# A down product of seven block products in four chunks, with the final norm at the end, and the first norm's root by groups

## The chip, the cores and the metric
One Trainium2 chip; the kernel runs on one of its cores. The metric is the device time of one execution in microseconds (us). The engines are TensorE (PE in the profile, PEld its weight loads), VectorE (DVE), ScalarE (ACT), GpSimd (POOL) and SyncE (SP), which only issues DMAs. DMAs go out from the queues of SP and of POOL.

## What is computed
One step of a hybrid encoder layer for 640 tokens (512 of a prompt, 8 streams of 16), width 2048, feed-forward width 5632:

```python
h = rmsnorm(x, norm1_g)
x = x + concat(GLA(h @ W_in), GatedDeltaNet(h @ W_in), RWKV7(h @ W_in)) @ W_out
h = rmsnorm(x, norm2_g)
x = x + (silu(h @ W_gate) * (h @ W_up)) @ W_down
y = rmsnorm(x, final_norm_g)        # y_prompt, y_sample
```

Everything is float32, and the mixers' states are outputs as well. Each large product is made in float32 by three matmuls: an operand is split into a part `hi`, which ACT copies in a rounded format, and the rest `lo`, which DVE subtracts; the product is hi·hi + hi·lo + lo·hi.

## The kernel before, in words
`build` (L1358) runs the stages one behind another. `norm1` (L1433) loads five tiles of 128 tokens, squares each on ACT, takes its root on DVE (`rsq`, twelve small operations), scales it on DVE (L1453 to L1457) and turns it on PE (L1464), so that features lie on partitions. `mixers` is ordered by a planner of its own, which the change does not touch. `outproj1` and `outproj2` multiply by `w_out`; in `outproj2` the sum x2 is kept feature-major, its squares feed the second norm, and `rows` (L1580) turns it on PE and stores it token-major in DRAM (`x2d`). From there on the tile scheduler fixes each engine's order; `high_priority(offset=WPRIO)` puts weight preparation ahead.

`gateup` (L1723) makes the gate and up products. Each of 21 pairs of matrices (256 columns) is made from seven block products in place of eight (Strassen and Winograd's scheme: the four quarters of the weights and of the activations, with four sums of each, `S1` to `S4` and `T1` to `T4`), 24 matmuls of 128x320 each (`pw`, L1736 to L1738); the first pair is made by the dense `first`. The products are added on DVE (L1744, L1779, L1784), and the activations s, 44 blocks of 128 features by 640 tokens, go to DRAM (`actd`).

`down` (L1795) multiplies them by `w_ffn_down` in five chunks of 9, 9, 9, 9 and 8 feature blocks. For each chunk it loads and splits the activations (L1811, L1812); for each of four column blocks of 512 it splits the weights (`split`, L1321, L1322) and runs the three matmuls of 128x512 per feature block and token tile (L1835 to L1837), 2,640 in all, into eight PSUM banks; DVE adds each bank to y in SBUF (L1839). In the last chunk ACT squares y as each column block is done (L1842), POOL multiplies three column blocks by the norm's weight (L1845), and for the last column block the order goes by token tile, so that root, scaling and the outputs of a tile (L1847 to L1858) follow while PE works on the next.

Of the kernel before, what the change touches and what calls it, by code (L numbers as in the profile page):

```python
# [11 lines left out]
F32 = mybir.dt.float32  # L12
# [8 lines left out]
T = 640  # L21
# [1264 lines left out]
class Trunk:  # L1286
# [10 lines left out]
    def split(self, src, shape, fill=None, keep=False):  # L1297
# [12 lines left out]
        with self.tc.high_priority(offset=WPRIO):  # L1310
# [5 lines left out]
            if keep:  # L1316
                hi, lo = (self.fb.tile(shape, F32R, name=self.name("k" + x), tag="k" + x, bufs=5) for x in ("h", "l"))
            else:
                hi = self.wp.tile(shape, F32R, name=self.name("hi"), tag="hi", bufs=NHL)
                lo = self.wp.tile(shape, F32R, name=self.name("lo"), tag="lo", bufs=NHL)  # L1320
# [39 lines left out]
    def build(self):  # L1360
        tc, nc, a, o = self.tc, self.nc, self.a, self.o
        ctx = ExitStack()
        with ctx:
            self.wp = ctx.enter_context(tc.tile_pool(name="wp", bufs=1))
# [7 lines left out]
            x2d = dp.tile([NT, 128, D], F32, name="x2d")  # L1372
            actd = dp.tile([44, 128, T], F32, name="actd")
            mctx = ExitStack()
            bp = ctx.enter_context(tc.tile_pool(name="bp", bufs=1, side="right"))
            self.free, self.where = [(bp, f"b{i}") for i in range(32)], {}
# [13 lines left out]
            self.px = ctx.enter_context(tc.tile_pool(name="px", bufs=1, space=PSUM))  # L1390
            with tc.tile_pool(name="fa", bufs=1) as self.fa:
                self.outproj2(KORDER[8:], xs, x2, self.col("norm2_g"), x2d, actd)
                self.gateup(actd)
            with tc.tile_pool(name="fb", bufs=1) as self.fb:
                self.down(actd, x2d)
# [27 lines left out]
    def norm1(self, h):  # L1423
        tc, nc, a = self.tc, self.nc, self.a
        with tc.tile_pool(name="xp", bufs=1) as xp, tc.tile_pool(name="xps", bufs=2, space=PSUM) as xps:
# [27 lines left out]
            for i in range(NT):  # L1453
                with tc.high_priority():
                    nc.scalar.activation(junk, xs[i], AF.Square, accum_out=ssq[:, i:i + 1])
                    r = self.rsq(xp, ssq[:, i:i + 1], 1, 1.0 / D)
                    nc.vector.tensor_scalar(xs[i], xs[i], r, None, ALU.mult)  # L1457
# [97 lines left out]
    def outproj2(self, ks, xs, x2, g2, x2d, actd):  # L1555

        nc, a, fa, px = self.nc, self.a, self.fa, self.px
# [21 lines left out]

        def rows(hf, q):  # L1580

            for t0, t1 in cuts[hf]:
                n, t = t1 - t0, 320 * hf + t0
                p = self.pe.tile([128, 512], F32, name=self.name("yt"), tag="e")
                for j in range(4):
                    nc.tensor.transpose(p[0:n, j * 128:(j + 1) * 128], xv[4 * q + j][:, t:t + n], self.ident)
# [307 lines left out]
```

## Time and profile before

| | us |
|---|---|
| three runs: median (lowest, highest) | 3337.22 (3337.09, 3342.08) |
| profiled execution, its own time | 3333.61 |
| its span | 3331.5 |
| PE busy | 3283.1 |
| DVE busy | 2037.4 |
| ACT busy | 1226.7 |
| POOL busy | 186.6 |
| clock granted to PE, mean | 0.994 |

The span runs from the first to the last instruction of the profiled execution. Busy time of an engine that others do not wait for costs nothing by itself. A matmul's record is longer than its place in the queue, since matmuls overlap.

### The profile page before, as it was taken

Reading aid. Unit: us, or ns where it says so; the run is one execution under the profiler, and the core shown is the slowest. Engines: PE = TensorE matmul, PEld = TensorE weight load, DVE = VectorE, ACT = ScalarE, POOL = GpSimd, SP = SyncE. Lnnn points to the kernel's source line nnn. Section 1 sums busy time; section 2 is a strip of 40 time slices with the busy share of each in tenths; the row PEclk is TensorE's granted clock in tenths of the full one; section 3 lists DMA queues with packets and bytes.
Section 4 is the critical chain, followed back from the end, with each engine's and each line's share of the span. In section 5 each row is a group of like instructions: output and inputs, shape, how many; then the busy total and the mean of one; then the engine's idle time right before and its main releaser. Section 6 shows DMA issues by size and latency. Waiting matters only on the chain.

```text
span 3331.5 us, 58063 instructions
## 1 busy us (share of the span) xinstructions
PE 3283.1 (99%) x22453; PEld 3042.1 (91%) x22453; DVE 2037.4 (61%) x5209; ACT 1226.7 (37%) x2593; POOL 186.6 (6%) x332
## 2 busy tenths in 40 slices
PE   6999999999999999999999999999999999999998
PEld 6988888899899999999999999999999988888886
DVE  5677577645666666426887777777777753233335
ACT  4433333323333334335543444444444332122123
POOL 1111111000100000002000000000000000000001
PEclk9999999999999999999999999999999999999999
DMA  4221121122222224435533333333323363233223
GB/s 127 57 52 49 45 52 42 49 59 75 75 73 72 76 73 134 131 106 176 146 99 93 100 102 100 98 97 105 105 85 105 105 215 105 83 108 98 80 83 114
DMA packets 357016, 312.08 MB, mean 94 GB/s; under 512 B 24161, under 2 KB 313427, under 8 KB 355971
## 3 DMA queue, kind: packets, MB, share of 16 engines
q1 hardware_dynamic: 347794, 287.97, 29.5%
q0 software_dynamic: 8656, 20.40, 2.1%
q8 instruction: 175, 2.87, 0.4%
q14 instruction: 103, 0.84, 0.1%
q10 hardware_dynamic: 288, 0.01, 0.0%
HBM read 271.32 MB, written 36.98 MB: 93 GB/s over the span
## 4 chain that ended last, share of the span: by engine, by line
PE 93%; DVE 3%; DMA 2%; ACT 1%; issue 1%; SPq 0%; ACTq 0%; DVEq 0%
PE d_r L292 23%; PE pw L1736 10%; PE pw L1737 10%; PE pw L1738 10%; PE mm_r L292 10%; PE dn L1835 6%; PE dn L1837 6%; PE dn L1836 6%; PE pd L1338 3%; PE pd L1339 3%; PE pd L1340 3%; PE ma_r L292 2%; PE po_r L292 1%; PE pd L1539 1%; DMA b<-mixd 0%
## 5 line engine op out<-in xcount | busy, mean ns | idle before, releaser
L292 PE MATMUL d_r<-b,hi_r 128*128 128x320 f32 (+1 forms) x3648 | 807.3, 319 | 0.7 <-ACT b L1471 0.7
L292 PEld LDWEIGHTS d_r<-b,hi_r 128*128 128x128 f32 (+1 forms) x3648 | 598.8, 189 | 23.9 <-issue 15.5
L292 PE MATMUL d_r<-b,lo_r 128*128 128x320 f32 (+1 forms) x1824 | 511.2, 319 | 0.0
L1322 DVE TENSOR_TENSOR lo<-raw,hi 128x512 fp32r<-128x512 f32 x299 | 210.3, 704 | 457.0 <-ACT hi L1321 441.8
L1736 PE MATMUL pw<-b,hi 128*128 128x320 f32 x1416 | 437.6, 309 | 0.0
L1737 PE MATMUL pw<-b,hi 128*128 128x320 f32 x1416 | 437.5, 309 | 0.0
L1738 PE MATMUL pw<-b,lo 128*128 128x320 f32 x1416 | 437.2, 309 | 0.0
L1321 ACT ACTIVATE hi<-raw 128x512 fp32r<-128x512 f32 x299 | 188.6, 631 | 540.0 <-PE dn L1837 388.8
L1835 PE MATMUL dn<-hi,b 128*128 128x512 f32 x855 | 338.5, 396 | 0.1
L1836 PE MATMUL dn<-lo,b 128*128 128x512 f32 x855 | 337.1, 394 | 0.4 <-DVE lo L1322 0.4
L1837 PE MATMUL dn<-hi,b 128*128 128x512 f32 x855 | 337.1, 394 | 0.0
L292 PEld LDWEIGHTS d_r<-b,lo_r 128*128 128x128 f32 (+1 forms) x1824 | 326.3, 189 | 10.8 <-issue 6.5
L1736 PE MATMUL pw<-b,hx 128*128 128x320 f32 x936 | 289.5, 309 | 0.0
L1737 PE MATMUL pw<-b,hx 128*128 128x320 f32 x936 | 289.2, 309 | 0.0
L1738 PE MATMUL pw<-b,lx 128*128 128x320 f32 x936 | 289.2, 309 | 0.0
L292 DVE TENSOR_TENSOR lo_r<-raw_r,hi_r 128x512 fp32r<-128x512 f32 (+1 forms) x228 | 155.3, 682 | 182.0 <-ACT hi_r L292 121.0
L1736 PEld LDWEIGHTS pw<-b,hi 128*128 128x128 f32 x1416 | 266.0, 188 | 0.4 <-ACT b L1576 0.2
L1737 PEld LDWEIGHTS pw<-b,hi 128*128 128x128 f32 x1416 | 266.1, 188 | 0.2
L1738 PEld LDWEIGHTS pw<-b,lo 128*128 128x128 f32 x1416 | 266.0, 188 | 0.0
L292 ACT ACTIVATE hi_r<-raw_r 128x512 fp32r<-128x512 f32 (+1 forms) x228 | 142.1, 624 | 243.4 <-PE d_r L292 206.9
L1338 PE MATMUL pd<-b,hi 128*128 128x320 f32 x640 | 201.0, 315 | 3.9 <-ACT s L1675 2.7
L1339 PE MATMUL pd<-b,hi 128*128 128x320 f32 x640 | 198.7, 311 | 0.4 <-DVE b L1514 0.4
(465 smaller groups left out, 5756.6 us busy)
## 6 DMA issues: line engine op xcount, KB each, us to landing
raw_r<-in_w_in SPq DMA_DIRECT2D x224, 256.0 KB
raw<-in_w_ffn_down SPq DMA_DIRECT2D x176, 256.0 KB
rw<-in_w_ffn_gate SPq DMA_DIRECT2D x84, 512.0 KB
rw<-in_w_ffn_up SPq DMA_DIRECT2D x84, 512.0 KB
raw<-in_w_out SPq DMA_DIRECT2D x80, 256.0 KB
actd<-s SPq DMA_DIRECT2D x88, 160.0 KB
b<-actd SPq DMA_DIRECT2D x44, 320.0 KB
mixd<-G_r POOLq DMA_DIRECT2D x16, 320.0 KB, 2.5
```

Of the source, the lines that this page charges most:

```text
L292: self.made.append(op[2](*op[3], **op[4]))
L1321: nc.scalar.activation(hi, raw, AF.Copy)
L1322: nc.vector.tensor_tensor(lo, raw, hi.bitcast(F32), ALU.subtract)
L1338: nc.tensor.matmul(out, lhsT=hi[:, kk, :], rhs=xh, start=k == 0, stop=False)
L1339: nc.tensor.matmul(out, lhsT=hi[:, kk, :], rhs=xl, start=False, stop=False)
L1340: nc.tensor.matmul(out, lhsT=lo[:, kk, :], rhs=xh, start=False, stop=k == nk - 1 and not extra)
L1736: nc.tensor.matmul(ps, lhsT=hi[:, kk, :], rhs=bh, start=k == 0, stop=False)
L1737: nc.tensor.matmul(ps, lhsT=hi[:, kk, :], rhs=bl, start=False, stop=False)
L1738: nc.tensor.matmul(ps, lhsT=lo[:, kk, :], rhs=bh, start=False, stop=k == 7)
L1835: nc.tensor.matmul(pds[i], lhsT=ah, rhs=hi, start=j == 0, stop=False)
L1836: nc.tensor.matmul(pds[i], lhsT=ah, rhs=lo, start=False, stop=False)
L1837: nc.tensor.matmul(pds[i], lhsT=al, rhs=hi, start=False, stop=j == len(fs) - 1)
```

## The change
`down` is written anew by the scheme of `gateup`. The 22 pairs of feature blocks are cut into four chunks of 5, 6, 6 and 5; per chunk and per block of 256 output columns (eight) seven products of 15 or 18 matmuls of 128x320 are made, 3,696 matmuls in all. The four quarters of the result are added by DMAs that accumulate into `yd`, feature-major in DRAM, where `outproj2` has stored x2 (32 stores; `rows` is gone). In the last chunk `load` and `turned` bring each finished block back, turn it on PE, square it on ACT and multiply it by the norm's weight on DVE. After the last block come one root for all five token tiles, 20 scalings and all 20 outputs.

The activations are stored as seven operands (four sums added by `store_sums`), loaded from POOL's queue two units at a time, and split in units of 128x320 by `Acts`, three products ahead of their use. Its first loads begin in the last up matrix, as each of that matrix's operands is given back.

In `norm1` the root is taken for tiles (0), (1, 2) and (3, 4) together, and the last tile is scaled on ACT. The pool `wp` moves and is closed before `down`; the tiles of `tq` and `s` live in a pool `fs` through the end.

```diff
-            for i in range(NT):
+            for i0, i1 in ((0, 1), (1, 3), (3, 5)):
                 with tc.high_priority():
...
+                    for i in range(i0, i1):
+                        nc.scalar.activation(junk, xs[i], AF.Square, accum_out=ssq[:, i:i + 1])
+                    r = self.rsq(xp, ssq[:, i0:i1], i1 - i0, 1.0 / D)
+                    for i in range(i0, i1):
+                        if i < NT - 1:
+                            nc.vector.tensor_scalar(xs[i], xs[i], r[:, i - i0:i - i0 + 1], None, ALU.mult)
+                        else:
+                            nc.scalar.activation(xs[i], xs[i], AF.Copy, scale=r[:, i - i0:i - i0 + 1])
...
+                nc.sync.dma_start(out=yd[m][:, c], in_=xv[m][:, c])
...
-                if m % 4 == 0 and m:
-                    rows(hf, m // 4 - 1)
...
+    def store_sums(self, m, s):
...
+        sub(t3, s[3], s[1])
+        sub(s[1], s[1], s[0])
+        sub(s[3], s[3], s[1])
+        sub(s[0], s[2], s[3])
+        for x, t in (("T3", t3), ("T1", s[1]), ("T2", s[3]), ("T4", s[0])):
+            nc.sync.dma_start(out=self.acts.at(x, m), in_=t)
...
+        def used(x):
+            self.give(*self.places[x])
+            self.acts.step(True)
...
+    def down(self, yd):
...
+        for n, (p0, p1) in enumerate(CHUNKS):
...
+                def split(x):
+                    hi, lo = tile("dh", F32R, pool=fw), tile("dl", F32R, pool=fw)
+                    nc.scalar.activation(hi, A[x], AF.Copy)
+                    nc.vector.tensor_tensor(lo, A[x], hi.bitcast(F32), ALU.subtract)
+                    return hi, lo
...
+                def product(parts, x):
...
+                    B = acts.take(n, x)
+                    for k in range(c):
+                        bh, bl = B[k][:, 0:320], B[k][:, 320:640]
+                        nc.tensor.matmul(ps, lhsT=hi[:, k], rhs=bh, start=k == 0, stop=False)
+                        nc.tensor.matmul(ps, lhsT=hi[:, k], rhs=bl, start=False, stop=False)
+                        nc.tensor.matmul(ps, lhsT=lo[:, k], rhs=bh, start=False, stop=k == c - 1)
...
+                with early():
+                    t1 = tq()
+                    d11 = split("11")
+                    total("S1", "21", "22", ALU.add)
+                    total("S2", "S1", "11", ALU.subtract)
+                    s2 = split("S2")
+                nc.scalar.activation(t1, product(d11, "11"), AF.Copy)
+                acts.step(p == 7)
...
+                u2, u4 = tq(), tq()
+                plus(u2, t1, product(s2, "T2"))
+                acts.step(p == 7)
...
+            def turned(p, y):
+
+                junk = tq()[:, 0:256]
                 for i in range(NT):
...
+                    ps = self.px.tile([128, 512], F32, name=self.name("yt"), tag=("st", "y")[i % 2])[:, 0:256]
+                    for j in range(2):
+                        nc.tensor.transpose(ps[:, 128 * j:128 * j + 128], y[j].bitcast(F32)[:, 128 * i:128 * i + 128], self.ident)
+                    nc.scalar.activation(junk, ps, AF.Square, accum_out=ssq[:, i, p:p + 1])
...
+                    nc.vector.tensor_tensor(rows[i, p // 2][:, 256 * (p % 2):256 * (p % 2) + 256], ps,
+                                            gf[p // 2][:, 256 * (p % 2):256 * (p % 2) + 256], ALU.mult)
...
+                def done(i, x, y):
+                    z = tq() if i == 3 else x
+                    plus(z, x, y)
+                    if last and p == 7:
+                        out = yl[i // 2].bitcast(F32)[:, ones(i)]
+                        plus(out, out, z)
                     else:
...
+                        nc.gpsimd.dma_start(out=yd[2 * p + i // 2][:, ones(i)], in_=z, accum_op=ALU.add)
...
+            turned(7, yl)
+            tot = fb.tile([128, NT], F32, name="ytot")
+            nc.vector.tensor_reduce(tot, ssq, AX.X, ALU.add)
+            r = self.rsq(fb, tot, NT, 1.0 / D)
...
+class Acts:
...
+    def step(self, many=False):
+
+        self.now += 1
+        free = self.trunk.free
+        for i in range(3):
+            if self.loaded and free and self.loaded[0][0] <= self.now - 7:
+                self.split()
+        soon = self.now + 3 - self.begin
+        if soon >= 0:
+            n, x = divmod(soon, 56)
+            if x < 7 and n < len(CHUNKS):
+                self.make(n, OPS[x])
+        for i in range(4 if many else 1):
+            if self.next < len(self.units) and len(free) > 2 and len(self.loaded) < (14 if many else 4):
+                self.load()
...
+CHUNKS = ((0, 5), (5, 11), (11, 17), (17, 22))
```

The order on ACT at the seam from `gateup` to `down`; before, the splits of the down product's activations (L1811) stand among weight splits of the last up matrix (`hi`, `hx`, L1710):

```order
L1710 ACTIVATE hi_28361<-rw_28235 128x512 [waits DMAHW7_49,PE_49,Activation_49]
L1811 ACTIVATE b_28523<-b_28525 128x640 [waits DMAHW4_49]
L1710 ACTIVATE hi_28393<-sx_28327 128x512 [waits DVE_49,PE_49,Activation_49]
L1811 ACTIVATE b_28529<-b_28531 128x640 [waits DMAHW5_49]
L1710 ACTIVATE hx_28397<-sx_28329 128x512 [waits DVE_49,PE_49,Activation_49]
L1811 ACTIVATE b_28535<-b_28537 128x640 [waits DMAHW6_49]
L1710 ACTIVATE hx_28431<-raw_28253 128x512 [waits PE_49,Activation_49]
```

With the change, the activation splits (L2001) stand ahead of the weights of the first products (`dh`, L1857; `dh_28597` is the first product's weight, `dh_28605` the second's):

```order
L1857 ACTIVATE dh_28597<-dr_28592 128x640 [waits DMAHW0_49]
L2001 ACTIVATE b_28899<-b_28721 128x320
L2001 ACTIVATE b_29267<-b_29086 128x320 [waits DVE_49]
L2001 ACTIVATE b_29080<-b_28902 128x320 [waits DMASW6_49,PE_49]
L2001 ACTIVATE b_29083<-b_28902 128x320 [waits PE_49]
L2001 ACTIVATE b_29110<-b_28932 128x320 [waits DMASW7_49]
L2001 ACTIVATE b_29113<-b_28932 128x320
L1857 ACTIVATE dh_28605<-ds_28603 128x640 [waits DVE_49]
L1857 ACTIVATE dh_28643<-ds_28601 128x640
L1857 ACTIVATE dh_28683<-dr_28594 128x640 [waits DMAHW2_49,PE_49,Activation_49]
L1886 ACTIVATE t_28596<-dn_28609 128x320 [waits PE_49]
```

The weight split of the second product moved behind four activation splits, two of which wait for transfers.

The order on DVE at the end of the program. Before, the last token tile's addition, reduce and root follow the scaling of the tile ahead of it:

```order
L1849 SCALAR_TENSOR_TENSOR b_28601<-b_28601,q_32823,gfrow 128x512 [waits DVE_49]
L1852 TENSOR_SCALAR b_28591<-b_28591,q_32823 128x512 [waits Pool_49]
L1839 TENSOR_TENSOR b_28603<-b_28603,dn_32567 128x512 [waits PE_49]
L1847 TENSOR_REDUCE yssq<-yssq 128x1 [waits Activation_49]
L1476 TENSOR_SCALAR q_32847<-yssq 128x1 [waits DVE_49]
L89 TENSOR_SCALAR q_32848<-q_32847 128x1 [waits DVE_49]
```

With the change, the last additions (L1826) and multiplications of turned tiles (L1941) stand ahead of one reduce (L1960) and one root for all tiles:

```order
L1941 TENSOR_TENSOR b_35049<-yt_35045,b_33443 128x256 [waits Activation_49]
L1826 TENSOR_TENSOR b_34898<-b_34898,t_34906 128x320 [waits DVE_49]
L1941 TENSOR_TENSOR b_35025<-yt_35070,b_33443 128x256 [waits Activation_49]
L1941 TENSOR_TENSOR b_35031<-yt_35075,b_33443 128x256 [waits Activation_49]
L1941 TENSOR_TENSOR b_35037<-yt_35080,b_33443 128x256 [waits Activation_49]
L1941 TENSOR_TENSOR b_35043<-yt_35085,b_33443 128x256 [waits Activation_49]
L1941 TENSOR_TENSOR b_35049<-yt_35090,b_33443 128x256 [waits Activation_49]
L1960 TENSOR_REDUCE ytot<-yssq 128x5
L1482 TENSOR_SCALAR q_35097<-ytot 128x5 [waits DVE_49]
```

The scaling of every tile moved behind the last product.

The order on ACT in norm 1, from the square of the fourth tile on, before and now (`x_129` is the last tile, `hi_r` a weight of the first mixer):

```order
L1455 ACTIVATE xjunk,xssq<-x_127 128x2048 [waits DMAHW1_49,Activation_49]
L1455 ACTIVATE xjunk,xssq<-x_129 128x2048 [waits DMAHW2_49,Activation_49]
L292 ACTIVATE hi_r_394<-raw_r_393 128x512 [waits DMAHW3_49]
L1471 ACTIVATE b_74<-xpa_234,cols_106 128x640 [waits PE_49]
L1471 ACTIVATE b_76<-xpa_242,cols_106 128x640 [waits PE_49]
```

```order
L1457 ACTIVATE xjunk,xssq<-x_127 128x2048 [waits DMAHW1_49,Activation_49]
L1457 ACTIVATE xjunk,xssq<-x_129 128x2048 [waits DMAHW2_49,Activation_49]
L1463 ACTIVATE x_129<-x_129,q_184 128x2048 [waits DVE_49,Activation_49]
L293 ACTIVATE hi_r_362<-raw_r_361 128x512 [waits DMAHW3_49]
L1477 ACTIVATE b_74<-xpa_202,cols_106 128x640 [waits PE_49]
```

The scaling of the last tile moved from DVE to ACT, ahead of the first weight's split.

## Rows read from the trace of the kernel before

**Rows 1.** The page: the span, PE's busy time, the chain's shares by engine.
```profile
span 3331.5 us, 58063 instructions
...
PE 3283.1 (99%) x22453; PEld 3042.1 (91%) x22453; DVE 2037.4 (61%) x5209; ACT 1226.7 (37%) x2593; POOL 186.6 (6%) x332
...
PE 93%; DVE 3%; DMA 2%; ACT 1%; issue 1%; SPq 0%; ACTq 0%; DVEq 0%
```

**Rows 2.** Table by stretches: start:end, us, busy time (count) by engine, PEclk, DMA share, GB/s.
```profile
2200.00:2600.00 400.00, 400.00 (x2727) 400.00 (x2726) 295.44 (x504) 163.85 (x275) 0.00 (x0) 1.00 0.33 100
...
2820.00:3220.00 400.00, 400.00 (x1720) 322.88 (x1719) 135.92 (x204) 89.22 (x139) 0.00 (x0) 1.00 0.30 93
...
3321.00:3324.00 3.00, 0.46 (x2) 0.02 (x1) 1.59 (x8) 1.01 (x3) 0.00 (x0) 1.00 0.82 299
```

**Rows 3.** PE's timeline at both ends of the down product: start us, us, line, operation.
```profile
2703.94 0.31 PE L1738 MATMUL pw<-b,lo 128*128 128x320 f32 x1
...
2704.08 0.40 PE L1835 MATMUL dn<-hi,b 128*128 128x512 f32 x1
...
3321.06 0.40 PE L1837 MATMUL dn<-kh,b 128*128 128x512 f32 x1
```

**Rows 4.** PE's timeline in the second out-projection, around twelve transposes.
```profile
1495.21 0.31 PE L1340 MATMUL pd<-b,lo 128*128 128x320 f32 x1
...
1495.36 1.47 PE L1586 MATMUL yt<-ident,b 128*128 128x128 f32 x12
...
1496.97 0.31 PE L1340 MATMUL pd<-b,lo 128*128 128x320 f32 x1
```

**Rows 5.** Timelines of ACT, DVE and PE in norm 1, its last tile.
```profile
16.52 1.91 ACT L1455 ACTIVATE xjunk<-x 128x2048 f32<-128x2048 f32 x1 [0.55 <-DMA x<-in_x_sample]
...
24.56 1.29 DVE L1457 TENSOR_SCALAR x<-x,q 128x2048 f32<-128x2048 f32 x1
...
25.91 0.69 PE L1464 MATMUL xpa<-ident,x 128*128 128x128 f32 x2 [2.82 <-DVE x L1457]
```

**Rows 6.** Timelines of DVE, ACT and SP after the last matmul.
```profile
3323.03 0.16 DVE L1847 TENSOR_REDUCE yssq<-yssq 128x1 f32<-128x4 f32 x1 [0.85 <-ACT yjunk L1842]
...
3325.53 0.72 ACT L1850 ACTIVATE b<-b,q 128x512 f32<-128x512 f32 x1 [2.53 <-DVE q L94]
...
3326.28 1.95 SPq L1858 DMA_DIRECT2D out_y_sample<-b  x4
```

**Rows 7.** Timelines of POOL and DVE where both work, in two stretches.
```profile
213.49 0.56 POOL L292 DMA_DIRECT2D mixd<-G_r  x1 [3.03 <-DVE G_r L292]
...
213.72 0.68 DVE L292 TENSOR_TENSOR KB_r<-a_r,a_r 128x512 f32<-128x512 f32 x1
...
3233.23 3.07 DVE L1839 TENSOR_TENSOR b<-b,dn 128x512 f32<-128x512 f32 x5
...
3234.76 7.22 POOL L1845 TENSOR_TENSOR b<-b,gfrow 128x512 f32<-128x512 f32 x5 [520.28 <-ACT yjunk L1842]
...
3236.22 1.64 DVE L1322 TENSOR_TENSOR lo<-raw,hi 128x512 fp32r<-128x512 f32 x1
```

**Rows 8.** DMA issues: transfer, queue, count, KB each, median us to landing.
```profile
mixd<-G_r POOLq DMA_DIRECT2D x16, 320.0 KB, 2.5
...
Ss_r<-in_state_gdn POOLq DMA_DIRECT2D x6, 512.0 KB, 5.0
```

**Rows 9.** DVE and ACT by line and form: count, busy us, mean ns.
```profile
L1744 DVE TENSOR_TENSOR tq<-tq,pw 128x320 f32<-128x320 f32 x98 | 47.7, 487 | 43.6 <-PE pw L1738 43.3
...
L1322 DVE TENSOR_TENSOR lo<-raw,hi 128x512 fp32r<-128x512 f32 x138 | 95.3, 691 | 279.9 <-ACT hi L1321 279.8
...
L1812 DVE TENSOR_TENSOR b<-b,b 128x640 fp32r<-128x640 f32 x28 | 23.1, 825 | 41.1 <-ACT b L1811 41.0
...
L1811 ACT ACTIVATE b<-b 128x640 fp32r<-128x640 f32 x28 | 20.7, 738 | 43.6 <-DMA b<-actd 43.2 <-DVE b L1812 0.3
```

More of the change, by code (lines that the diff above doesn't have):

```diff
@@ L1 @@
 import heapq
+import itertools
 import math
@@ L1315, in split @@
                 nc.sync.dma_start(out=view, in_=ap)
[L1316 to L1320, printed above, removed]
+            hi = self.wp.tile(shape, F32R, name=self.name("hi"), tag="hi", bufs=NHL)
+            lo = self.wp.tile(shape, F32R, name=self.name("lo"), tag="lo", bufs=NHL)
             nc.scalar.activation(hi, raw, AF.Copy)
@@ L1578, in split @@
             ops[x].append(out)
[L1580 to L1586, printed above, removed]
-                row = self.take()
-                nc.scalar.activation(f(row)[0:n, 0:512], p[0:n], AF.Copy)
-                nc.sync.dma_start(out=x2d[t // 128][t % 128:t % 128 + n, q * 512:(q + 1) * 512], in_=f(row)[0:n, 0:512])
-                self.give(row)
         def first(k):
@@ L1652, in outproj2 @@
             split(new("T2"), v[:, H], "T2")
-        self.first(actd)
+        self.first()
         self.give(*b12)
@@ new lines, with __init__, at, load @@
+class Acts:
+    def __init__(self, trunk, actd):
+        self.trunk, self.actd = trunk, actd
+        self.units = [(n, x, p) for n, (p0, p1) in enumerate(CHUNKS) for x in OPS for p in range(p0, p1)]
+        self.now, self.next, self.loaded, self.made = 0, 0, [], {}
+        self.begin = 7
+    def at(self, x, p):
+        return self.actd[[u[1:] for u in self.units].index((x, p))]
+    def load(self):
+        i = self.next
+        self.next += 2
+        place = self.trunk.take()
+        raw = place.bitcast(F32).rearrange("p (q c) -> p q c", q=2)
+        self.trunk.nc.gpsimd.dma_start(out=raw, in_=self.actd[i:i + 2].rearrange("q p c -> p q c"))
+        for q in range(2):
+            self.loaded.append((self.now, *self.units[i + q][:2], raw[:, q], place if q else None))
+    def split(self):
+        nc = self.trunk.nc
+        at, n, x, raw, place = self.loaded.pop(0)
+        t = self.trunk.take()
+        hi, lo = t[:, 0:320], t[:, 320:640]
+        nc.scalar.activation(hi, raw, AF.Copy)
+        nc.vector.tensor_tensor(lo, raw, hi.bitcast(F32), ALU.subtract)
+        self.made.setdefault((n, x), []).append(t)
+        if place is not None:
+            self.trunk.give(place)
+    def step(self, many=False):
[12 more added lines that the diff above has]
+                self.load()
+    def make(self, n, x):
+        p0, p1 = CHUNKS[n]
+        while len(self.made.get((n, x), [])) < p1 - p0:
+            if not self.loaded:
+                self.load()
+            self.split()
+    def take(self, n, x):
+        self.make(n, x)
+        return self.made[n, x]
+    def used(self, n, x):
+        self.trunk.give(*self.made.pop((n, x)))
```

230 lines of the change are left out of this document (138 added, 92 removed).

## The prediction
> **What bounds the kernel now.** I read the page first. PE is busy 99% of a span of 3331.5 us, DVE 61%, and the chain of waits is 93% PE [rows 1]: a change pays by what it takes off PE's queue, and costs where another engine makes PE wait. The table by stretches then gives a price per matmul. In 400 us of the gate and up products PE issues 2727 matmuls of 128x320, 0.1467 us each; in 400 us of the down product 1720 of 128x512, 0.2326 us each [rows 2]. Both are full queues, PE busy the whole 400 us at clock 1.00, so start-to-start is the price (the records' own lengths overlap). PE's timeline gives the ends of the stage: the last `pw` starts at 2703.94, the first `dn` 0.14 us later, the last `dn` at 3321.06 [rows 3]. The stage is 617.1 us, and 2,640 x 0.2326 = 614.1 fills it: down has nearly no stalls to win back, only matmuls.
>
> **The down product.** The order has 3,696 matmuls of 128x320 in place of 2,640 of 128x512: 8 output blocks x 7 products x 22 pairs x 3. At 0.1467 that is 542.2, so **-71.9 us**. The price is that of the gate and up stage, whose form is the same (three matmuls per 128x128 weight, 320 columns). Bounds: 0.1467 in that stage, and 0.1454 if 0.2326/512 held per column (-76.8).
> The Trainium skill (TensorE: Matmul & The Clock Gate, "Back-to-back issue gap") gives sustained spacings of about 81 ns at 128 columns and 131 ns at 512, that is a large part that does not shrink with the columns, which speaks against cutting matmuls narrower. The two rows here, 147 ns and 233 ns, lie 0.45 ns per column apart with some 3 ns left over [rows 2], so the trace does not agree.
>
> **Transposes taken from the second out-projection.** `rows` turns x2 there: 96 transposes. In PE's timeline twelve stand between the matmuls that start at 1495.21 and 1496.97 [rows 4]; of these 1.76 us three matmuls of 0.147 take 0.44, so twelve transposes take 1.32, 0.11 us each. **-10.6 us**. The 24 ACT copies went beside matmuls; 32 stores on SP replace 24, no load waits for them.
>
> **Norm 1.** x's last tile is squared at 16.52 on ACT, but its root waits behind tile 3's on DVE, and its scaled form comes at 24.56 + 1.29; PE's last such wait is 2.82 us, ended at 25.91 [rows 5]. With tiles 3 and 4 in one root, twelve operations at 0.19 us from about 18.6 follow tile 2's scaling; I place the last tile's end at about 22.9, on ACT beside tile 3 on DVE. **-2.9 us**, bounds 0 (another wait takes its place) and -3.5 (one whole root and scaling).
>
> **Turning the result in the last chunk.** 80 transposes, 70 of them among the last chunk's matmuls at 0.11: **+7.7 us**. Their 35 Squares and 35 multiplications are in the load below.
>
> **The tail.** Now, 10.2 us pass from the end of the last matmul (3321.06 + 0.23) to 3331.5: an addition, a Square, a reduce and root (3323.03 to 3325.53), scaling, four outputs of 256 KB [rows 6]; the other 16 outputs went out before. Afterwards all 20, 5.24 MB, follow the one root. Terms: last additions 1.2; the last ten transposes with their five Squares and multiplications through two PSUM banks, 3.75; reduce and root 2.5; first scaling 0.7; issue 0.4; 5.24 MB at 299 GB/s, the rate of the stretch that writes these rows now [rows 2], 17.5; landing of the last about 2.4, what four outputs take beyond their bytes at the end now. Sum 28.5, so **+18.3 us**. The share in that stretch is 0.82: at a full share 365 GB/s would save 3 us; at half the rate of 299 for the first few, 6 more. Bounds +12 and +24.
>
> **Stalls that come.** At the seam from gate/up to down, ACT's queue holds four splits of activations (`b_29080` to `b_29113`) ahead of `dh_28605`, the weight of the second product. Their two loads stand on POOL's queue behind PE's last gate/up product, whose places they use. A load is 0.56 us of issue [rows 7], some 4.3 us to landing (320 KB took 2.5, 512 KB 5.0, [rows 8]), two splits of 0.38 and one of 0.75: 7.2 us after PE's last `pw`, less the first product, 15 x 0.1467 = 2.2: 5.0 us. At each of three chunk seams the next weights and splits meet in the same way, but loads are three products ahead: 2 us each by choice. In the last chunk 2 us for transposes waiting for a bank. **+13 us**. The trace of before shows no such queue, so the bounds are far: 2 (all hidden, as the seam now, 0.14 us [rows 3]) and 40 (5 to 10 us at each seam, the first product's cover gone).
>
> **DVE's load, costed at nothing.** This is the cover that can go. Five additions of 128x512 take 3.07 us, 0.61 apart [rows 7]; widths 512 and 640 differ by 0.134 [rows 9]; so by spacing 0.41 for 320 columns, 0.74 for 640, 0.87 for 768 (estimates from these rows). A weight block of six pairs needs 7 splits and 4 sums of 768 (9.6), 7 additions (2.9) and 5.25 activation splits (2.2): 14.6 of PE's 18.5 us. With five pairs 13.2 of 15.4. On the whole about 445 of 550 us, 81%, against 74% in gate/up now [rows 2], where PE has no stall. At the first chunk's start it is 39.6 of 41.8 us, which is why seams are priced. ACT (0.74 us for 640 columns, [rows 9]) has seven splits, a copy and the activation splits, some 8 of 18.5 us. DMA moves under 200 GB/s, and 299 is seen [rows 2].
>
> **Sum.** -71.9 - 10.6 - 2.9 + 7.7 + 18.3 + 13 = -46.4. The profiled execution took 3333.6 us (span 3331.5); the median of the runs is 3337.2, 3.6 more. Against the median: **3291 us**.
>
> **Rivals.**
> 1. *DVE sets the pace at seams and in the five-pair chunks.* If each operation cost its whole recorded length (0.825 for 640 columns, 0.487 for 320 [rows 9]), a five-pair block needs 15.0 of 15.4 us, and any wait for ACT or a transfer goes straight to PE. For: DVE's order is fixed, and its operations wait for ACT's. Against: the gate and up stage holds 74% with no stall. Stalls of 26 to 57 in place of 13: 3304 to 3335.
> 2. *Slower: POOL's DMA issues hold DVE.* In the last chunk of before, a DVE subtraction beside a POOL TENSOR_TENSOR took 1.64 us rather than 0.69 [rows 7]. The change issues 201 DMAs from POOL in this stage (124 that add to `yd`, 77 loads). If each held DVE 0.95 us, 191 us come on DVE, whose room is 105: 86 us longer, 3377. It decides from 0.52 us each; slower than before from 0.79. Against: an addition of 128x512 at 213.72 that ran beside a POOL DMA issue kept its 0.68 us [rows 7]. The Trainium skill (SBUF — State Buffer, "Who interferes with whom") says that an operation with two SBUF inputs contends with a GpSimd operation that reads SBUF, and that `tensor_tensor` does not starve descriptor writing; both rows agree.
> 3. *Matmuls have a large fixed part.* If a 128x320 matmul in down cost what interpolation between a small and a wide form would leave it, it would be 0.166 us in place of 0.1467 to eat the 72 us; the stage now runs 2727 of that form in 400 us [rows 2], so nothing speaks for it but another operand layout (weights 128 columns within a longer row). 3363 at that price.
> The Trainium skill's spacings (TensorE: Matmul & The Clock Gate, "Back-to-back issue gap") would make it, as an estimate, 106 ns against 131, 46 us more rather than 72 less, 3409.
> 4. *Cheaper than forecast.* The scheduler hides the seams (2 to 4 us in all) and the outputs leave at 365 GB/s: 3276.
> 5. *The change does not do what it says*, for instance a chain of additions to the same rows of `yd` that holds the `t` tiles: nine tiles, four per block, two blocks or 30 us until reuse against landings of 2.5 to 5 us [rows 8]. A wait of that kind would give back most of the gain, some 3330.
>
> **How the numbers follow.** Forecast 0.72 (its own range 3278 to 3304), rival 1 0.14, rival 2 0.05, rival 3 0.01, rival 4 0.07, rival 5 0.01. The range 3275 to 3314 leaves out half of rival 4's spread below, the upper half of rival 1, and rivals 2, 3 and 5: about 0.18. A measurement tells some 0.2%, 6.7 us, from no change: faster is below 3330.5, slower above 3343.9. Forecast, rival 4 and most of rival 1 (0.10) are faster: 0.89; a rest of rival 1 and rival 5, 0.04; rivals 2, 3 and a share of unforeseen stalls, 0.07.
>
> **What would show it.** PE's rows of `dn` 128x320 should come to 0.147 us start-to-start in a table of 100 us stretches, 3,696 of them, and the stage to some 563 us from the last `pw` to the last `dn`, with 70 transposes in it. PE's waits should name ACT `dh` once at the first seam with about 5 us. PE's last wait in norm 1 should end near 23. After the last PE instruction about 25 us, most of them with PE, DVE and ACT idle and DMA's share near 0.8. The prediction is wrong if PE waits for DVE `dl` in each block (rival 1), if DVE operations beside POOL issues are longer than 0.7 (rival 2), or if the tail is outside 22 to 34 us.

## The result and the profile after

| | before | changed |
|---|---|---|
| runs taken together: median (lowest, highest), us | 3339.65 (3337.09, 3342.94) | 3301.34 (3294.08, 3307.97) |
| profiled execution, us | 3333.61 | 3307.97 |
| its span, us | 3331.5 | 3306.2 |

The ratio is 0.9889, 95% interval 0.9874 to 0.9904: 38.3 us faster by the medians, where 46.4 were forecast, and 3301.34 lies inside the range, some 10 us above the 3291. The profiled execution of the change is the slowest of its four runs, so the two profiles are only 25.3 us of span apart. The balance below is that of the profiles.

The page after, against [rows 1]:

```profile
span 3306.2 us, 61295 instructions
...
PE 3228.6 (98%) x23493; PEld 3099.3 (94%) x23493; DVE 2309.0 (70%) x5677; ACT 1322.8 (40%) x2797; POOL 330.7 (10%) x521
...
PE 85%; issue 5%; DVE 4%; DMA 3%; POOL 1%; ACT 1%; SPq 0%; POOLq 0%; DVEq 0%; ACTq 0%
```

PE's share of the chain fell from 93% to 85%: the path now leaves PE. PE's timeline after, at the marks at which the two profiles are compared ([rows 3], [rows 5]); the bracket is PE's wait and what ended it:

```profile
22.50 1.47 PE L1470 MATMUL xpa<-ident,x 128*128 128x128 f32 x4 [3.13 <-DVE x L1461]
...
1646.49 0.64 PE L1338 MATMUL pd<-b,lo 128*128 128x320 f32 x1 [2.47 <-DVE lo L1320]
...
2700.33 0.31 PE L1749 MATMUL pw<-b,lo 128*128 128x320 f32 x1
2705.69 0.63 PE L1873 MATMUL dn<-b,dh 128*128 128x320 f32 x1 [5.06 <-ACT dh L1857]
...
2706.98 0.47 PE L1873 MATMUL dn<-b,dh 128*128 128x320 f32 x1
...
2709.92 0.47 PE L1875 MATMUL dn<-b,dl 128*128 128x320 f32 x1
2711.47 0.41 PE L1873 MATMUL dn<-b,dh 128*128 128x320 f32 x1 [1.08 <-ACT dh L1857]
...
2827.93 0.41 PE L1873 MATMUL dn<-b,dh 128*128 128x320 f32 x1 [1.30 <-ACT dh L1857]
...
3280.43 0.39 PE L1875 MATMUL dn<-b,dl 128*128 128x320 f32 x1
```

| part of the span, us | before | after | difference | forecast |
|---|---|---|---|---|
| up to the first `pw` | 1667.08 | 1663.13 | -3.9 | -13.5 (norm 1, transposes) |
| first to last `pw` | 1036.9 | 1037.2 | +0.3 | 0 |
| last `pw` to last `dn` | 617.1 | 580.1 | -37.0 | -51.2 (matmuls, transposes, stalls) |
| after the last `dn` | 10.2 | 25.6 | +15.4 | +18.3 |

The main loss is in the third line. The table by stretches after (columns as in [rows 2]) shows where it is:

```profile
2680.00:2700.00 20.00, 20.00 (x138) 20.00 (x137) 19.84 (x46) 16.71 (x42) 12.61 (x18) 1.00 0.95 309
...
2706.00:2710.00 4.00, 4.00 (x15) 3.62 (x14) 1.81 (x4) 2.02 (x5) 0.00 (x0) 0.50 1.04 374
...
2720.00:2800.00 80.00, 80.00 (x548) 80.00 (x547) 71.23 (x122) 32.05 (x51) 21.94 (x26) 1.00 0.66 144
2820.00:2840.00 20.00, 18.39 (x122) 17.57 (x121) 13.56 (x24) 11.20 (x25) 11.68 (x16) 1.00 0.86 259
...
2980.00:3000.00 20.00, 15.47 (x95) 14.52 (x96) 16.08 (x30) 14.20 (x33) 9.82 (x13) 0.94 0.90 264
...
3120.00:3140.00 20.00, 18.11 (x122) 17.59 (x121) 11.71 (x20) 8.63 (x17) 10.43 (x14) 1.00 0.93 257
```

In the 80 us inside the first chunk PE is never idle: they hold 548 matmuls, 0.146 us each, with DVE at 89%. At the four seams (from gate/up, and between chunks) PE is short, and the DMA engines are at 0.86 or more of their time. The start-to-start spacing of PE's rows over 0.147 us, added up at each seam, is 9.4, 6.8, 8.3 and 4.1 us: 28.6. With 542.2 for the matmuls and 7.7 for the transposes that leaves 1.6 of the 580.1 for everything else.

How the first seam's 9.4 us come about can be read from the rows above. The first `dn` starts 5.2 us late. Its 15 matmuls follow at the granted clock 0.50 (1.2 GHz, the lower of the two levels): from 2706.98 to 2709.92 eleven steps of 0.267 us, and 4.5 us for the product in place of 2.2, 2.3 more. Then the second product starts 1.3 us later than it could. PE's waits from 2690 to the end (total, times, longest):

```profile
PE dn L1873 <- ACT dh L1857: 14.7, 7, 5.1
PE dn L1875 <- DVE dl L1858: 3.0, 5, 1.2
```

They come to 17.7 of the seams' 28.6 us; the rest is slow matmuls and gaps too small to be listed. ACT's timeline at the first seam:

```profile
2700.74 0.83 ACT L2001 ACTIVATE b<-b 128x320 fp32r<-128x320 f32 x2 [2.66 <-DMA b<-actd]
2703.41 1.60 ACT L2001 ACTIVATE b<-b 128x320 fp32r<-128x320 f32 x4 [1.84 <-DMA b<-actd]
2704.92 0.72 ACT L1857 ACTIVATE dh<-dr 128x640 fp32r<-128x640 f32 x1
```

ACT waits twice for loaded activations, and the weight's split `dh`, on which PE waits, stands behind. It is that of the first product's weight, `dh_28597` of the order on ACT: six splits stand between it and the next `dh`, as they do there. Its own weights had landed at 2700.93, so it started 4.0 us after they were there.

The second product's `dh` waits for something else. ACT was idle for 2.02 us ahead of it, since the sums `ds` on DVE, from which it is made, waited for the second load of weights:

```profile
2708.68 0.82 DVE L1863 TENSOR_TENSOR ds<-dr,dr 128x640 f32<-128x640 f32 x1 [2.19 <-DMA dr<-in_w_ffn_down]
...
2710.68 1.37 ACT L1857 ACTIVATE dh<-ds 128x640 fp32r<-128x640 f32 x2 [2.02 <-DVE ds L1863]
```

That load of 640 KB was issued by SP at 2696.08 and had landed at 2708.66, 12.6 us later. So the wait that ends last at the first seam is one for weights, late in the same crowd of transfers, and not one for activations. At the seams between chunks both kinds of wait of ACT ahead of `dh` occur, for loads and for PE, whose finished product gives back the buffer that a split writes (by the code):

```profile
2826.78 0.47 ACT L2001 ACTIVATE b<-b 128x320 fp32r<-128x320 f32 x1 [4.92 <-DMA b<-actd]
...
2979.07 1.37 ACT L2001 ACTIVATE b<-b 128x320 fp32r<-128x320 f32 x3 [6.02 <-PE dn L1875]
```

In the DMA view, the loads over the whole span, and all traffic from 2676 to 2712 with the loads in it (to landing in us at the end):

```profile
b<-actd POOLq DMA_DIRECT2D x77, 320.0 KB, 6.6
yd<-t POOLq DMA_DIRECT2D x124, 160.0 KB, 4.8
```

```profile
DMA packets 5143, 11.23 MB, mean 312 GB/s; under 512 B 516, under 2 KB 3604, under 8 KB 5140
...
b<-actd POOLq DMA_DIRECT2D x24, 320.0 KB, 5.3
```

In 36 us, 24 of the 77 loads go out beside the last activations' stores and the first weights, since that is when `gateup` gives its buffers back.

### The profile page after: what moved, and what is told of

It reads as the page before. It is cut to its first block, busy times and chain, and to the rows that moved or that the text cites. A ratio compares the mean times of both kernels' runs of the same rounds, so it can differ in the third digit from the quotient of the medians.

```text
span 3306.2 us, 61295 instructions
## 1 busy us (share of the span) xinstructions
PE 3228.6 (98%) x23493; PEld 3099.3 (94%) x23493; DVE 2309.0 (70%) x5677; ACT 1322.8 (40%) x2797; POOL 330.7 (10%) x521
## 4 chain that ended last, share of the span: by engine, by line
PE 85%; issue 5%; DVE 4%; DMA 3%; POOL 1%; ACT 1%; SPq 0%; POOLq 0%; DVEq 0%; ACTq 0%
PE d_r L293 23%; PE pw L1747 10%; PE pw L1748 10%; PE pw L1749 10%; PE mm_r L293 10%; PE dn L1875 3%; PE dn L1873 3%; PE dn L1874 3%; PE pd L1336 3%; PE pd L1338 3%; PE pd L1337 3%; PE ma_r L293 2%; DMA b<-actd 1%; PE po_r L293 1%; POOL yd L1953 1%
## 5 line engine op out<-in xcount | busy, mean ns | idle before, releaser
L1873 PE MATMUL dn<-b,dh 128*128 128x320 f32 x1232 | 384.7, 312 | 14.8 <-ACT dh L1857 14.7
L1875 PE MATMUL dn<-b,dl 128*128 128x320 f32 x1232 | 384.3, 312 | 3.1 <-DVE dl L1858 3.0
L1874 PE MATMUL dn<-b,dh 128*128 128x320 f32 x1232 | 383.4, 311 | 0.0
L1873 PEld LDWEIGHTS dn<-b,dh 128*128 128x128 f32 x1232 | 233.6, 190 | 17.0 <-ACT dh L1857 17.0
L1875 PEld LDWEIGHTS dn<-b,dl 128*128 128x128 f32 x1232 | 233.5, 190 | 5.9 <-DVE dl L1858 5.6
L1874 PEld LDWEIGHTS dn<-b,dh 128*128 128x128 f32 x1232 | 233.4, 189 | 0.0
L1336 PE MATMUL pd<-b,hi 128*128 128x320 f32 x640 | 202.7, 318 | 2.1 <-ACT s L1668 1.5
```

The lines of the kernel that those rows point to most:

```text
L1336: nc.tensor.matmul(out, lhsT=hi[:, kk, :], rhs=xh, start=k == 0, stop=False)
L1873: nc.tensor.matmul(ps, lhsT=hi[:, k], rhs=bh, start=k == 0, stop=False)
L1874: nc.tensor.matmul(ps, lhsT=hi[:, k], rhs=bl, start=False, stop=False)
L1875: nc.tensor.matmul(ps, lhsT=lo[:, k], rhs=bh, start=False, stop=k == c - 1)
```

## The experiments

The expectations weigh theory A, that the seams' cost comes from the activations' loads (they land late, their splits wait, and `dh` waits behind them on ACT), against other ends of the same wait: the weights' own traffic, the load of ACT and DVE, the accumulating stores. "The stretch" is from the start of the last `pw` to that of the last `dn` in the profiled execution: 617.1 before, 580.1 with the change. Ratios are against the kernel before, run on the same chip.

**The loads left out.**
```diff
-        place = self.trunk.take()
-        raw = place.bitcast(F32).rearrange("p (q c) -> p q c", q=2)
-        self.trunk.nc.gpsimd.dma_start(out=raw, in_=self.actd[i:i + 2].rearrange("q p c -> p q c"))
+        if i == 0:
+            place = self.trunk.take()
+            self.old = place.bitcast(F32).rearrange("p (q c) -> p q c", q=2)
+            self.trunk.nc.gpsimd.dma_start(out=self.old, in_=self.actd[i:i + 2].rearrange("q p c -> p q c"))
+        raw, place = self.old, None
```


> The changed kernel with the first of the 77 activation loads alone; every split reads it, so the output is not the reference's, while all 154 splits on ACT and DVE, all weights, matmuls and stores stay. The first run of this kind kept a wait, since a split took a place into which a load was still going; here there is no load to wait for. Theory A: PE's waits for dh fall from 14.7 under 4 us and the stretch from 580.1 to 552 to 566. Theory B: waits of 10 to 16 and 575 to 583.

Stretch 554.5, median 3279.26, ratio 0.9829 [0.9804, 0.9854]. PE's timeline at both ends and all its waits from 2690 on (total, times, longest):

```profile
2696.52 0.31 PE L1749 MATMUL pw<-b,lo 128*128 128x320 f32 x1
...
2697.69 0.41 PE L1873 MATMUL dn<-b,dh 128*128 128x320 f32 x1 [0.86 <-ACT dh L1857]
...
3250.99 0.39 PE L1875 MATMUL dn<-b,dl 128*128 128x320 f32 x1
```

```profile
PE yt L1937 <- DVE b L1941: 2.3, 3, 0.9
PE dn L1873 <- ACT dh L1857: 1.4, 2, 0.9
PE dn L1875 <- DVE dl L1858: 0.4, 1, 0.4
```

The loads cost 25.6 us of the stretch. Every split, addition, weight and accumulating store is still there, so the amount of work on ACT and DVE is not what holds the seams; and 554.5 is 542.2 + 7.7 + 4.6, so the prices of matmul and transpose stand. Taking the loads away takes away their landing, their share of the queues (DVE's `ds` waits 0.3 us for weights here, 5.4 with the change) and the buffers that they fill (ACT's splits wait 0.8 us for PE here, 12.2 with the change): which of the three matters is not told by this run.

**The splits read a tile that is already there, with the loads still made.**
```diff
+        if not hasattr(self, "old"):
+            self.old, place = raw, None
+            self.loaded[0] = (*self.loaded[0][:4], None)
+        raw = self.old
```


> The changed kernel, but every activation split of the down product reads the tile of the first load that landed; all 77 loads are still made, so the output is not the reference's. Traffic, the splits on ACT and DVE and nearly the order stay; only the wait of a split for its own load is gone. Theory A (weight splits stand on ACT behind activation splits whose loads land late): the waits of PE for dh, 14.7 us in the changed kernel, fall under 5, the stretch from the last pw to the last dn falls from 580.1 to 560 to 568, the whole by 12 to 20 us. Theory B (the seams are short of ACT and DVE time): waits and stretch stay within 3 us.

Stretch 588.7, median 3307.14, ratio 0.9907 [0.9885, 0.9928]. It was meant to take the wait and leave the traffic. But a split writes into a buffer that another load had only just been sent to, and the wait moved there; ACT's waits say so:

```profile
ACT b L2005 <- DMA b<-actd: 35.1, 14, 7.3
```

The changed kernel has 24.2 us of them. Nothing follows for either theory.

**Half the weights' loads left out.**
```diff
+                    if p % 2:
+                        r = kept[j]
...
+                        continue
-                    r = tile("dr", F32, 256, 4)
+                    r = kept[j] = tile("dr", F32, 256, 4)
```


> The changed kernel with the weights of down loaded for every second block of columns only, and used for two blocks (so half of the result is another block's product); 32 loads of 640 or 768 KB rather than 64, all matmuls, splits and activation loads as they were. Theory A1 (the loads are late because weights and activations fill the DMA queues at the seams): landing of a 320 KB activation load at the chunk seams falls from 7 to 8 us towards 4 to 5, PE's waits for dh fall to 4 to 9, the stretch to 566 to 574. Theory A2 (late because of POOL's issue order and the accumulating stores): landing stays over 6.5 and the stretch within 3 us of 580.

Stretch 578.6, median 3302.88, ratio 0.9882 [0.9861, 0.9902]; PE's waits for `dh` 14.2 us (14.7 with the change). The loads still take 6.6 us. The weights of the stretch as a whole are not the cause; those of the first block behind a seam are still loaded here, so this run does not tell their part at the seam itself, which the second product's wait above shows for the first seam.

**Splits two products ahead, and four.**
```diff
-        soon = self.now + 3 - self.begin
+        soon = self.now + 2 - self.begin
```


> The changed kernel with the activations made two products ahead of their use rather than three. Theory A: the loads go out as before and the splits stand one product (2.2 to 2.6 us) later on ACT, so less of a late load is waited for ahead of dh: PE's waits for dh 5 to 11, the stretch 570 to 577. Theory B: splits come later at places short of ACT and DVE time, the stretch 580 to 588.

> The changed kernel with the activations made four products ahead. Theory A: splits stand ahead of loads that landed even less, so PE's waits for dh rise to 18 to 26 and the stretch to 584 to 592. Theory B: the work is spread over more products, the stretch 570 to 579.

Stretch 583.7 and 581.3, medians 3306.72 and 3303.44, ratios 0.9901 [0.9878, 0.9924] and 0.9885 [0.9863, 0.9907]. The 570 to 577 that theory A gave for two ahead did not come, and four ahead met neither forecast. The distance in the program does little either way. That the tile scheduler, which sets the order, does not follow the distance would explain it; it is not shown.

**Fewer loads before the seam.**
```diff
-            if self.next < len(self.units) and ...
+            if self.next < (len(self.units) if self.now >= self.begin else 36) and ...
```


> The changed kernel, but until the last product of gate and up only the 36 units that the first chunk of down and its last load need are loaded; the eight loads for the second chunk that stood among them come later. Theory A (transfers are late at the seam): the first dh and the second block's weights no longer stand behind those loads, so PE's first wait falls from 5.1 us under 2, what the first seam costs from 9.4 to 2 to 5, the stretch from the last pw to the last dn from 580.1 to 572 to 577. Theory B (ACT and DVE time): the work of the splits that the first products need is the same, the first wait stays 4 to 6 us and the stretch within 3 us.

Stretch 577.8, median 3301.35, ratio 0.9898 [0.9879, 0.9917]. PE's first wait is 5.5 us, where it was 5.1. A miss and no test: the scheduler brought the later loads forward on POOL, and 24 of them went out in the 36 us around the seam, as many as with the change.

**Accumulating stores in the first chunk only.**
```diff
-                        nc.gpsimd.dma_start(out=yd[2 * p + i // 2][:, ones(i)], in_=z, accum_op=ALU.add)
+                        if n == 0:
+                            nc.gpsimd.dma_start(out=yd[2 * p + i // 2][:, ones(i)], in_=z, accum_op=ALU.add)
```


> The changed kernel with the accumulating stores into yd for the first chunk of down only (so the second and third chunk's part of the result is left out); 64 of 124 go. Theory A with full queues at the seams: the stores take about a fifth of the 16 DMA engines at the chunk seams, so loads land some 1 to 2 us sooner, PE's waits at the second and third chunk seam fall by a third to a half, the stretch to 570 to 577. Rival (POOL's DMA issues hold DVE, rival 2 of the prediction): DVE's operations of 640 columns, 0.82 us in the changed kernel, get shorter, and the stretch falls in proportion to the stores, not at the seams alone. Theory B: within 3 us.

Stretch 575.7, median 3291.68, ratio 0.9869 [0.9843, 0.9895]. The edit takes out more than the expectation says: the fourth chunk's stores go too, and 32 of the 124 are left. The third and fourth seam cost 4.5 us in all where the changed kernel's cost 12.4. The second, with its stores, is as it was (7.1 against 6.8). The first, which no accumulating store precedes, cost 12.8 against 9.4, so some 3 us at one seam can come from elsewhere than the edit; the 8 us at the last two are more than that. The stores are a part of the crowd at the later seams. DVE's operations keep their length, with 139 stores and loads issued by POOL in this stretch or with 82, which is rival 2's test. By line and form (count, busy, mean ns), the changed kernel and this one, from 2720 to 3130:

```profile
L1826 DVE TENSOR_TENSOR t<-t,dn 128x320 f32<-128x320 f32 x160 | 75.5, 483 | 34.1 <-PE dn L1875 34.1
...
L1858 DVE TENSOR_TENSOR dl<-dr,dh 128x640 fp32r<-128x640 f32 x22 | 18.1, 822 | 2.5 <-ACT dh L1857 1.9
```

```profile
L1858 DVE TENSOR_TENSOR dl<-dr,dh 128x640 fp32r<-128x640 f32 x20 | 16.5, 823 | 2.4 <-ACT dh L1857 1.9
```

**Each load as two of half the size.**
```diff
-        self.trunk.nc.gpsimd.dma_start(out=raw, in_=self.actd[i:i + 2].rearrange("q p c -> p q c"))
         for q in range(2):
+            self.trunk.nc.gpsimd.dma_start(out=raw[:, q], in_=self.actd[i + q])
```


> The changed kernel with each activation load made as two DMAs of 160 KB, 154 issues on POOL rather than 77. If the weights (dr, rows of 1 KB) come late at the first seam because they share each queue by turns with activation packets five times as large, smaller packets help them: the first seam from 9.4 us to 4 to 7 and the stretch 572 to 577. If it is the sum of the bytes: within 3 us of 580. If POOL's issues (0.72 us each) are short: over 583.

Stretch 591.6, median 3309.60, ratio 0.9928 [0.9900, 0.9955]. Each lands sooner than the pair did, and PE waits longer, 8.2 us at the first seam:

```profile
b<-actd POOLq DMA_DIRECT2D x154, 160.0 KB, 4.1
```

So the time from issue to landing is not all that counts. POOL issues twice as many loads here, one behind another, and was busy 20.4 of the 24 us ahead of the last `pw`, where it was 15.9 with the change; that fits the longer wait but isn't told apart from other causes.

**The loads issued by SP.**
```diff
-        self.trunk.nc.gpsimd.dma_start(out=raw, in_=self.actd[i:i + 2].rearrange("q p c -> p q c"))
+        self.trunk.nc.sync.dma_start(out=raw, in_=self.actd[i:i + 2].rearrange("q p c -> p q c"))
```


> The changed kernel with the activation loads issued on SP's queue beside the weights' rather than on POOL's. If POOL's part matters (its 0.72 us per load, loads that stand behind stores into yd): the loads land 1 to 3 us sooner and the stretch falls to 566 to 576. If the sum of the bytes at the seams decides: 576 to 584. If SP's order is worse (loads behind a weight load that waits for its ring): over 586.

> The kernel with the activation loads on SP's queue once more, in five rounds, since its stretch of 572.3 us came from one profiled execution and the executions of one program differ by 6 to 15 us. If the gain is the kernel's: a stretch from the last pw to the last dn of 570 to 575 again, the first seam without a wait over 2 us, a ratio to the kernel before of 0.985 to 0.989. If it was that execution's: a stretch of 577 to 584.

Stretch 572.3 and 574.0, medians 3295.35 and 3296.57, ratios 0.9874 [0.9843, 0.9905] and 0.9876 [0.9853, 0.9898]. The first seam costs 4.8 and 3.9 us, where it cost 9.4 with the change and 10.8 to 16.2 in the other runs that make all loads from POOL. In the first of the two:

```profile
2695.93 0.31 PE L1749 MATMUL pw<-b,lo 128*128 128x320 f32 x1
...
2696.55 0.41 PE L1873 MATMUL dn<-b,dh 128*128 128x320 f32 x1 [0.30 <-ACT dh L1857]
```

The seams between chunks remain. Of the versions that do all the work this has the lowest median, some 5 us below the changed kernel, but the intervals overlap. One thing that changed can be read off: the order. In both runs no load goes out in the last 7 us ahead of the last `pw`, where five do with the change, and the weights' second load lands 6.8 us after its issue, not 12.6. How much of the gain is this, and how much issue time, is open: both change at once.

**More buffers for split weights.**
```diff
-                    r = tile("dr", F32, 256, 4)
+                    r = tile("dr", F32, 256, 3)
...
-                    hi, lo = tile("dh", F32R, pool=fw), tile("dl", F32R, pool=fw)
+                    hi, lo = tile("dh", F32R, pool=fw, bufs=4), tile("dl", F32R, pool=fw, bufs=4)
```


> The changed kernel with rings of four rather than three for the weights' parts (dh, dl) and of three rather than four for the loaded weights (dr), the same memory. Theory A with ACT's queue as the place (dh stands behind activation splits whose loads are late, so a deeper ring lets dh stand a product further ahead): PE's waits at the three chunk seams fall from 10 us to 0 to 4, the first seam stays at 8 to 12, the stretch from the last pw to the last dn from 580.1 to 566 to 574. Rival (the operands themselves come late, so that it does not matter where dh stands): the stretch stays at 576 to 584. With a shorter dr ring at fault: new waits for dr and over 584.

Stretch 594.8, median 3315.87, ratio 0.9936 [0.9912, 0.9959]. PE's waits changed sides:

```profile
PE dn L1875 <- DVE dl L1858: 15.0, 8, 3.9
PE dn L1873 <- ACT dh L1857: 7.8, 4, 5.2
```

Two sizes changed at once, but DVE's waits tell which one costs:

```profile
DVE ds L1863 <- DMA dr<-in_w_ffn_down: 99.6, 31, 7.0
```

With the change there are 5.4 us of them, 5 times. The longest, 7.0 us at 2782.71, ends just ahead of PE's wait of 3.9 us for `dl` at 2784.33. So the ring of raw weights, made shorter to make room, starts the weights' loads too late, as the expectation had it for a stretch over 584. What deeper rings for `dh` and `dl` do by themselves is not told.

**Loads earlier, and all splits at the seam.**
```diff
-            if self.loaded and free and self.loaded[0][0] <= self.now - 7:
+            if self.loaded and free and self.loaded[0][0] <= self.now - 60:
...
-            if ... len(self.loaded) < (14 if many else 4):
+            if ... len(self.loaded) < (28 if many else 28):
```


> The changed kernel with the activations of the next chunk kept unsplit, two units to a place, until three products before their use, so that 25 units rather than 15 have landed when the last block of a chunk begins and 17 rather than 27 are left to load in it (both read off the program's order); the splits then all stand at the seam, 42 in place of 27 or so. Bytes, issues and work are the same in sum. Theory A (the loads crowd at the seam): the second to fourth seam fall from 21 us together to 8 to 14, though the first may rise by some us, since more loads start there; the stretch from the last pw to the last dn 570 to 578. Rival (DVE short of time at the seams, rival 1 of the prediction): 17 us of splits on DVE in one seam give PE new waits for dl and dh, the stretch 583 to 600.

Stretch 587.8, median 3311.81, ratio 0.9912 [0.9883, 0.9941]. The waits for late loads shrink on ACT (24.2 us to 5.6, one wait) and new ones come on PE:

```profile
PE dn L1873 <- ACT dh L1857: 13.2, 4, 6.0
PE dn L1874 <- DVE b L2002: 5.8, 11, 1.0
PE yt L1937 <- DMA b<-yd: 5.0, 2, 2.7
```

The loss is at the first seam, which costs 16.2 us where it cost 9.4, and it hangs on weights there, not on splits: `dh` and `ds` wait for them, and PE 6.0 and 4.8 us behind.

```profile
2702.87 0.74 ACT L1857 ACTIVATE dh<-dr 128x640 fp32r<-128x640 f32 x1 [4.92 <-DMA dr<-in_w_ffn_down]
...
2710.45 0.82 DVE L1863 TENSOR_TENSOR ds<-dr,dr 128x640 f32<-128x640 f32 x1 [5.83 <-DMA dr<-in_w_ffn_down]
```

The other three seams together cost 13.8 us where they cost 19.2, inside the 8 to 14 that theory A gave; in what is left of them stand the 11 waits for DVE's splits of activations, 5.8 us, the rival's mechanism. The 5.0 us for blocks brought back from `yd` come on top, in the last chunk. So earlier loads helped the seams for which they had landed, and cost more where they stood in front of the first weights.

## Why the prediction was right or wrong

- **Matmuls, -71.9: right.** 80 us of the changed kernel hold 548 of them, and without the loads the stretch is within 4.6 us of price times count for matmuls and transposes. The Trainium skill (TensorE: Matmul & The Clock Gate, "Back-to-back issue gap") led to an estimate of 106 ns against 131; 146 ns here against the 233 of [rows 2] do not agree with it, as before.
- **Norm 1, -2.9: right.** The first `d_r` starts at 24.64, not 27.26: -2.6. PE's last long wait ends at 22.50 (near 23 was forecast).
- **Transposes, -10.6: right where they were, but counted past the next limit.** The second out-projection takes 116.5 us from its first `pd` to the first of the dense `first`, where it took 128.3: -11.9. From there to the first `pw` 5.1 us are given back (66.1 against 61.1), nearly all at the end of `first`. PE now comes earlier to a place where DVE is all but full (9.06 of 10 us, before 9.99), waits 2.47 us for `lo` at 1646.49, whose `hi` on ACT had itself waited 0.91 us for its weights, and goes on at the lower clock:

```profile
1640.00:1650.00 10.00, 7.00 (x35) 6.48 (x35) 9.06 (x21) 3.41 (x7) 0.00 (x0) 0.79 0.27 76
```

  The sum let a gain on PE's queue run through to the end without asking which engine is next. In the 12 runs of the changed kernel's variants the last piece takes 63.6 to 66.1 us, so a part of the loss is there each time.
- **Not in the sum: 9.1 us at the end of the mixers.** From the last `d_r` (1308) to the 201st `pd` (1367), in code that the change leaves alone, this execution lost 9.1 us on before's. From the first `d_r` to the last it gained 3.6 (1283.4 against 1287.0). The lower clock was granted for a time, PE being busy:

```profile
1346.00:1352.00 6.00, 6.00 (x53) 4.42 (x52) 0.00 (x0) 0.54 (x2) 0.00 (x0) 0.50 0.01 3
```

  Before had 1.00 there:

```profile
1350.00:1360.00 10.00, 10.00 (x94) 8.53 (x93) 1.85 (x4) 4.18 (x13) 0.00 (x0) 1.00 0.10 28
```

  The piece at the mixers' end took 50.1 us before and 59.3 after, but in the 12 runs of variants, whose code is the same up to there, it took 50.2 to 56.2, and the median of all 13 is 53.1. So some 6 of the 9.1 us are this execution's, which is a part of why the profiled pair shows less gain than the medians. From the first `d_r` to the last the 13 take 1279.3 to 1289.0, with before's 1287.0 among them. With one profile of before, whether the change has a part in the other 3 us stays open.
- **Stalls, +13: the step that failed.** The seams cost 28.6 us where 11 of the 13 were put on them, though inside the far bounds of 2 to 40. That the first wait came as forecast, 5.06 us against 5.0, is luck. The forecast took the first product's weight as ready, with 2.2 us of matmuls as cover, and asked when the second's, `dh_28605`, would be: 7.2 us after the last `pw` (its terms as named add up to 6.4). In the run PE waited for the first product's own `dh`, behind splits that the sum did not count, and `dh_28605` came 11.1 us after the last `pw`, held by the load of weights, which the sum for this seam had at nothing. The activations' loads were put at 4.3 us, between two rows of a quiet queue [rows 8], and took 6.6. "Under 200 GB/s" was right for the stage's mean (163 from 2695 to 3275); at the seams the rows show 257 to 374. And the three seams between chunks were set to 2 us each by choice, where 6.8, 8.3 and 4.1 came, of which a part is not waiting but matmuls at the lower clock after a wait, for which the sum had no term. By the run without loads, 25.6 us of the stretch hang on the activations' loads; how much of it by their late splits, by weights that come late beside them, or by buffers is not told apart.
- **Rival 1, DVE sets the pace: not here.** PE waits 3.0 us for `dl` in the whole stretch, and DVE's work is unchanged in the run without loads. DVE's load was estimated rightly, at 81%: it was busy 464.3 of the 580 us from 2695 on, 80%. It is close behind, though: at 89% inside the first chunk, and PE waits 5.8 us for its activation splits when they are put together (the last experiment).
- **Rival 2, POOL's issues hold DVE: refuted**, 483 and 822 ns beside them against 487 and 825 [rows 9]. The Trainium skill (SBUF — State Buffer, "Who interferes with whom") names, for an operation with two SBUF inputs, a GpSimd instruction that reads SBUF as the one it contends with, and says of `tensor_tensor` that a probe did not show it stalling DMA. The 822 ns agree with that.
- **Tail, +18.3: right, 2.9 too much.** The last additions and transposes took longer than forecast, 6.1 us to the reduce at 3286.66 rather than 5.0; the outputs took less:

```profile
3286.66 0.18 DVE L1960 TENSOR_REDUCE ytot<-yssq 128x5 f32<-128x40 f32 x1
...
3289.30 4.40 ACT L1967 ACTIVATE b<-b,q 128x512 f32<-128x512 f32 x7 [3.01 <-DVE q L95]
...
3289.82 9.97 SPq L1970 DMA_DIRECT2D out_y_prompt<-b  x16
```

```profile
3296.00:3300.00 4.00, 0.00 (x0) 0.00 (x0) 0.00 (x0) 0.00 (x0) 0.00 (x0) 0.50 1.01 380
```

  From the first output at 3289.82 to the end at 3306.2 are 16.4 us, where 19.9 were forecast (17.5 + 2.4): with 20 transfers queued the DMA share is full, at 380 GB/s, and not the 299 of four. Of the signs named, the tail of 25.6 us is within 22 to 34, but 20.5 us and not about 25 pass after the last PE instruction.

## What to carry to other kernels

Price a seam between stages by the traffic and the order at that seam, not by the stage's mean: where loads can only start as buffers come free, they start together, and with stores and weights they fill the queues just when the next stage needs its first operands, its weights among them. On an in-order engine, look at what stands ahead of the first small operation that PE waits for, and of the second; and count a wait of PE as longer than itself, since matmuls behind it may run at the lower clock. A gain on one engine's queue can end at the next place where another engine is full. A number that comes out as forecast is no proof of its reason: look which operation waited.

## What the runs showed that was not expected

- A wait of 5 us is followed by a whole product at the lower clock: 2706 to 2710 at 0.50, 0.267 us per matmul rather than 0.147. At the mixers' end it is 0.50 while PE is busy all of 1346 to 1352; a wait for DVE of 1.69 us at 1340.45 lies ahead of that. The kernel before had such a wait, 1.48 us at 1344.57, and kept 1.00.
- Loads of half the size that land in 4.1 rather than 6.6 us made the kernel slower (591.6 against 580.1), and the same loads from SP's queue faster (572.3 and 574.0).
- Outputs alone on the queues leave at 380 GB/s, about as fast as the mixed traffic of the first seam (374 from 2706 to 2710).
- A weights' load of 640 KB took 12.6 us in the crowd at the first seam, and 6.8 us when the activations' loads went out from the same queue as it.
